# The order of a mixer's parts, and the beat of a scan behind weight splits

## The chip, the cores and the metric

The kernel runs on one core of a Trainium2 chip. The metric is the device time of one execution in microseconds (us). Three executions of the kernel before are compared; one further execution was profiled. TensorE (PE) does matrix products, VectorE (DVE) and ScalarE (ACT) elementwise work, GpSimd (POOL) some of it and the start of some transfers, SyncE (SP) the start of most others.

## What is computed

A network of two blocks on 256 tokens of width 1024. In the first block each of two layers has a feed-forward net, a mixer and another feed-forward net; the second block (attention, a dense net, eight experts) is not touched here. The mixer projects its input to many parts with one weight matrix, runs two branches and adds them through gates:

```python
def s5_branch(u, ...):                       # one of the two branches
    bu = einsum("blgc,gnc->blgn", ug, b_bar)             # complex input to 64 states
    _, states = associative_scan(combine, (a_elems, bu)) # s_t = lam_bar * s_(t-1) + bu_t
    y = real(einsum("blgn,gcn->blgc", states, c)) + d_skip * uf
    y = gelu(y)
    val, gate = split(y @ w_glu, 2)
    return val * sigmoid(gate)

def mixer(u, w_in, ...):
    proj = u @ w_in
    z, xbc, dt_raw, u5, g_a, g_b = split(proj, SPLITS)
    y_a = ssd_branch(z, xbc, dt_raw, ...) @ w_branch_a   # conv, silu, chunked scan, gate, norm
    y_b = s5_branch(u5, ...) @ w_branch_b
    merged = sigmoid(g_a) * y_a + sigmoid(g_b) * y_b
    return merged @ w_out
```

The SSD branch has four groups of heads. For each group a causal convolution and a silu give `xs`, a silu gives `zs`, a masked product over two chunks of 128 tokens gives `yT`, which is gated by `zs`, normed over the group's 512 columns and split for the product with `w_branch_a`.

## The kernel before

Matrix products run in fp32 with operands split in two: a weight tile `raw` of 128x1024 is loaded, ScalarE casts it to `hi` (line 1576) and VectorE makes `lo = raw - hi` (line 1577, `unit`). Three products (`hi*xh`, `lo*xh`, `hi*xl`, lines 1591 to 1593) stand for one. Such a tile with its two parts is called a unit here. Parts have a ring of buffers (`hi`/`lo` 0 to 2 and a pair called `part`), so ScalarE and VectorE can be at most four units ahead of TensorE in the stretch that matters here. A projection onto 512 columns (`stream_b`) is four units of 24 products, 96 in all, into four of five accumulators (`acc...`); the next projection needs them emptied, by ScalarE and VectorE.

The mixer's work is cut into parts, and `ORDER` says in which order they are written:

- `p0` to `p3`: the projections of SSD group 0 to 3 (`ssd_proj`), first 512 columns for `xs` (emptied by a ScalarE step at line 566, three convolution steps on VectorE at line 569, a silu), then 512 for `zs` (silu, line 642): eight units each. `accpa` is p0's accumulator, `accpb` p1's, `accpc` p2's, `accpd` p3's.
- `d`: the projection for dt, one small unit, and a chain of small VectorE steps on `cut` tiles.
- `g0` to `g3`: the projections of the gates, four units each (`accga` to `accgd`), with a tanh on ScalarE (line 753).
- `c0` to `c3`: the cores of SSD group 0 to 3 (`ssd_core`, `ssd_gate`; accumulators `trca` to `trcd`). A core transposes `xs`, builds for each of four head pairs a mask `M` (VectorE line 681, exp on ScalarE lines 688 and 689, VectorE line 690), multiplies it (lines 695, 696), then gates: `yT*zs` (VectorE 708), a square (ScalarE 710), two halving sums (GpSimd 713), a product with ones (TensorE 715), a power (GpSimd 720), a scaled identity `dg` (VectorE 724) and a product with it (TensorE 725). Each step needs the one before.
- `o0` to `o3`: S5's outputs for a quarter of its groups each: products into `zoa` to `zod` (lines 494 to 496, with coefficients `s5CF` loaded by GpSimd's queue), a gelu on ScalarE and VectorE, transposes (`troa` to `trod`, line 515), a split into `g`.

After `ORDER` follow the products with `w_glu` (`accgl`, which read the four `g`), `w_branch_b` (`accmb`), `w_branch_a` (`accma`). A scheduler then mixes the instructions: cores and outputs are put between the products of later projections, so that TensorE, which runs its queue in order, has other work while a core's chain runs on the other engines.

S5's recurrence (`s5_rec`) is 28 VectorE instructions on `S`, 14 for each half of the groups: six multiplications and additions of 128x1024 (line 545), two scans (line 549), six more. They are not written as one piece. `stream_b` calls `beside` after each unit, and `beside` puts one of them behind that unit's split:

```python
    def beside(self):
        with self.tc.issue_after(self.last_lo):
            next(self.side, None)
```

`o0` and `o1` need the first half, `o2` and `o3` the second. `MIXER` says which of the numbered buffers each kind of tile takes in turn; "X" serves the gates' tiles, S5's coefficients and its outputs, "W" (2 and 3) the recurrence's two temporaries `s5x`.

Of the kernel before, what the change touches and what calls it, by code (L numbers as in the profile page):

```python
# [27 lines left out]

ORDER = "p0 d p1 g0 g1 o0 o1 p2 c0 g2 c1 p3 o2 o3 g3 c2 c3".split()

MIXER = {
    "X": [2, 3, 0, 1], "U": [4, 5], "A": [12, 13, 6, 7, 8, 9, 10, 11, 12, 13, 6, 7, 8, 9, 6, 7], "M": [15, 16],
    "E": [10, 11, 14], "W": [2, 3],
    "bc": ["h0", "h1"], "T": ["h2", "h3"],
}
# [24 lines left out]
class Quads:  # L64


    def __init__(self, tiles):
        self.tiles = tiles
# [10 lines left out]
class Mixer:  # L79
# [471 lines left out]

    def beside(self):

        with self.tc.issue_after(self.last_lo):
            next(self.side, None)

# [231 lines left out]
    def mixer_body(self, I, l, xh, xl, hd):  # L788
        v = self.nc.vector
        W = I["w_in"][l]  # L790
        pr, ys = {}, []

        def proj(g):
            pr[g] = self.ssd_proj(W, l, g, xh, xl)

        def core(g):
            xs, zs = pr.pop(g)
            yT = self.ssd_core(l, g, xs, BC, acd, col)
            return self.ssd_gate(l, g, yT, zs)

        u = self.s5_in(W, xh, xl)
        self.ring_drop(("S", 0), ("S", 1), (6, 7))
        self.once = []
        St = self.qp.tile([P, 2, 32, 64], F32, tag="S", name=self.nm("S"), bufs=1)
        self.nc.gpsimd.memset(St[:, :, :, 0:1], 0.0)
        d = [self.s5_put(u[0])]
        BC = [self.ssd_bc(W, l, 0, xh, xl)]
        U = self.s5_get(d[0])
        d.append(self.s5_put(u[1]))
        E = self.s5_tables(l, 0, self.nc.sync)  # L810
        for q in range(2):
            self.s5_z(q, U[q], St)
        BC.append(self.ssd_bc(W, l, 1, xh, xl))
        U += self.s5_get(d[1])
        for q in range(2, 4):
            self.s5_z(q, U[q], St)
        self.side = itertools.chain(self.s5_rec(St, l, 0, E), self.s5_rec(St, l, 1))
        self.ring.append((12, 13))
        g5, ds, y23 = [], [], []
        for w in ORDER:  # L820
            k, i = w[0], int(w[1:] or 0)
            self.at = k + "abcd"[i]
            if k == "p":
                proj(i)
            elif k == "d":
                acd, col, cols = self.ssd_dt(W, l, xh, xl)
            elif k == "c":
                if i == 1:
                    self.ring_drop((12, 13))
                with self.tc.issue_after(self.last_mm):  # L830
                    if i == 0:
                        cols()
                    y = core(i)
                if i < 2:
                    ys.append(self.ssd_split(y))
                else:
                    y23.append(y)
            elif k == "g":
                ds.append(self.gate_out(W, i, xh, xl))
            elif k == "o":  # L840
                if i == 0:
                    self.ring_drop((8, 9))
                with self.tc.issue_after(self.last_mm):
                    self.s5_out(i, U[i], St, g5)
        self.at = "gl"
        bs = self.glu(I["s5_w_glu"][l], g5)
        self.at = "mb"
        ys += [self.ssd_split(y) for y in y23]
        yh, yl = Quads([y[0] for y in ys]), Quads([y[1] for y in ys])
        bh, bl = Quads([b[0] for b in bs]), Quads([b[1] for b in bs])  # L850
        mT = []
        for c in range(0, D, 256):
            if c % 512 == 0:
                mT.append(self.gate_back(ds[c // 512]))
            bb = self.stream_b(I["w_branch_b"][l][:, c : c + 256], bh, bl)
            for i in range(2):
                m = mT[-1][:, (c // P + i) % 4]
                v.scalar_tensor_tensor(m, m, 1.0, bb[i][:, :S], op0=ALU.add, op1=ALU.mult)
        self.ring = [0, 1, 2]
        self.ring_add([("S", 0), ("S", 1), (4, 5), (15, 16)])  # L860
        self.at = "ma"
        ms = []
        for c in range(0, D, 256):
            if c % 512 == 0:
                ms.append([self.slot4("X", "ms", F32R) for _ in range(2)])
                tg = self.gate_back(ds[2 + c // 512])
            ab = self.stream_b(I["w_branch_a"][l][:, c : c + 256], yh, yl, nk=16)
            for i in range(2):
                k = (c // P + i) % 4
                m, g = mT[c // 512][:, k], tg[:, k]  # L870
                v.scalar_tensor_tensor(g, g, 1.0, ab[i][:, :S], op0=ALU.add, op1=ALU.mult)
                v.tensor_tensor(m, m, g, op=ALU.add)
                self.split_half(ms[-1][0][:, k], ms[-1][1][:, k], m)
        h = [self.slot("B", "h") for _ in range(2)]
        for t in range(2):
            self.nc.sync.dma_start(h[t], hd[t * P : (t + 1) * P, :])
        return self.stream_k(I["w_out"][l], Quads([m[0] for m in ms]), Quads([m[1] for m in ms]), 8), h
# [545 lines left out]
class Net(Mixer, Second):  # L1423
    def __init__(self, ctx, tc):
        self.tc = tc
        nc = self.nc = tc.nc
        self.n = 0
        self.at = ""
        self.ring = [0, 1, 2]
        self.once = []  # L1430
        self.side = iter(())
        self.Ed = {}
        self.hold = []
        self.chain = [[], []]
        self.last_tr = None
        self.raws = itertools.repeat(None)

        def pool(name, bufs, **kw):
            return ctx.enter_context(tc.tile_pool(name=name, bufs=bufs, **kw))

        self.const = pool("const", 1)
        self.raw = pool("raw", 4)
        self.hi = pool("hi", 1)
        self.lo = pool("lo", 1)
        self.xp = pool("xp", 1)
        self.s4 = pool("s4", 5)
        self.qp = pool("numbered", 1)
        self.sm = pool("sm", 8)
        self.dram = pool("dram", 2, space=DRAM)
        self.acc = pool("acc", 5, space=PSUM)  # L1450
        self.trp = pool("trp", 2, space=PSUM)
        self.zp = pool("zp", 1, space=PSUM)

        self.ones = self.const.tile([P, P], F32, name="ones")
        nc.vector.memset(self.ones, 1.0)
        self.ident = self.const.tile([P, P], F32, name="ident")
        make_identity(nc, self.ident)
        self.mhalf = self.const.tile([P, 1], F32, name="mhalf")
        nc.vector.memset(self.mhalf, -0.5)
# [529 lines left out]
```

## Time and profile before

| | before |
|---|---|
| median of 3 runs | 2934.55 us (2931.49 to 2935.66) |
| profiled execution | 2936.55 us, span 2934.5 us |
| TensorE busy | 2814.3 us (96%), weight loads 2508.2 us (85%) |
| VectorE, ScalarE, GpSimd busy | 2181.6 us (74%), 1674.2 us (57%), 206.0 us (7%) |
| granted TensorE clock, mean | 0.981 of full speed |

TensorE is busy nearly all the time, so what can be won or lost is the idle time between its instructions, and stretches at the lower of its two clock levels. The mixer comes twice, once for each layer; the part around the change lies at 304 to 524 us and again at 1116 to 1337 us.

### The profile page before, as it was taken

Reading aid. Unit: us, or ns where it says so; the run is one execution under the profiler, and the core shown is the slowest. Engines: PE = TensorE matmul, PEld = TensorE weight load, DVE = VectorE, ACT = ScalarE, POOL = GpSimd, SP = SyncE. Lnnn points to the kernel's source line nnn. Section 1 sums busy time; section 2 is a strip of 40 time slices with the busy share of each in tenths; the row PEclk is TensorE's granted clock in tenths of the full one; section 3 lists DMA queues with packets and bytes.
Section 4 is the critical chain, followed back from the end, with each engine's and each line's share of the span. In section 5 each row is a group of like instructions: output and inputs, shape, how many; then the busy total and the mean of one; then the engine's idle time right before and its main releaser. Section 6 shows DMA issues by size and latency. Waiting matters only on the chain. (4 is left out here: it accounts for less than half of the span.)

```text
span 2934.5 us, 49144 instructions
## 1 busy us (share of the span) xinstructions
PE 2814.3 (96%) x19040; PEld 2508.2 (85%) x19040; DVE 2181.6 (74%) x3043; ACT 1674.2 (57%) x2389; POOL 206.0 (7%) x257
## 2 busy tenths in 40 slices
PE   8979999999999999999999999999999999999997
PEld 7968888999979888888999898987678888888886
DVE  5886877765667758777755566555589999999997
ACT  5434456545445444475554445445377777777776
POOL 2140001000004100010000000000000000000000
PEclk9999999999999999999999999999899999999998
DMA  7677565576567775656855646654589999999993
GB/s 238 199 250 242 160 204 164 197 227 188 184 223 249 241 221 174 194 155 196 264 171 180 215 154 192 186 192 132 184 279 356 343 361 361 343 359 356 354 344 145
DMA packets 350928, 687.88 MB, mean 234 GB/s; under 512 B 32672, under 2 KB 121952, under 8 KB 350688
## 3 DMA queue, kind: packets, MB, share of 16 engines
q1 hardware_dynamic: 336592, 637.42, 65.9%
q0 software_dynamic: 13952, 46.74, 4.8%
q8 instruction: 151, 2.47, 0.3%
q14 instruction: 89, 0.73, 0.1%
q10 hardware_dynamic: 144, 0.52, 0.0%
HBM read 658.05 MB, written 26.54 MB: 233 GB/s over the span
## 5 line engine op out<-in xcount | busy, mean ns | idle before, releaser
L1577 DVE TENSOR_TENSOR lo<-raw,hi 128x1024 fp32r<-128x1024 f32 x646 | 788.6, 1230 | 296.8 <-ACT hi L1576 285.1
L1576 ACT CAST hi<-raw 128x1024 fp32r<-128x1024 f32 x646 | 674.9, 1048 | 455.6 <-PE accmo L1587 84.6
L1586 PE MATMUL accmo<-lo,xg 128*128 128x512 f32 (+1 forms) x768 | 289.7, 378 | 2.3 <-DVE lo L1577 2.3
L1587 PE MATMUL accmo<-hi,xg 128*128 128x512 f32 (+1 forms) x768 | 285.2, 372 | 0.0
L1585 PE MATMUL accmo<-hi,xg 128*128 128x512 f32 (+1 forms) x768 | 274.0, 373 | 1.4 <-ACT hi L1576 1.4
L1577 DVE TENSOR_TENSOR big<-raw,big 128x1024 fp32r<-128x1024 f32 x147 | 184.9, 1259 | 110.2 <-ACT big L1576 109.3
L1576 ACT CAST big<-raw 128x1024 fp32r<-128x1024 f32 x147 | 153.7, 1049 | 168.0 <-issue 31.1
L1577 DVE TENSOR_TENSOR part<-raw,part 128x1024 fp32r<-128x1024 f32 x111 | 135.3, 1223 | 85.5 <-ACT part L1576 83.1
L1576 ACT CAST part<-raw 128x1024 fp32r<-128x1024 f32 x111 | 116.1, 1050 | 114.2 <-DMA raw<-in_ffn_w_gate_dram 17.4
L1586 PEld LDWEIGHTS accmo<-lo,xg 128*128 128x128 f32 x768 | 144.6, 188 | 32.3 <-DVE lo L1577 5.6
L1585 PEld LDWEIGHTS accmo<-hi,xg 128*128 128x128 f32 x768 | 144.6, 188 | 28.1 <-ACT hi L1576 2.6
L1587 PEld LDWEIGHTS accmo<-hi,xg 128*128 128x128 f32 x768 | 144.8, 189 | 22.5
L1586 PE MATMUL accmo<-lo,th 128*128 128x512 f32 x352 | 138.0, 392 | 0.0
L1587 PE MATMUL accmo<-hi,th 128*128 128x512 f32 x352 | 137.7, 391 | 0.0
L1577 DVE TENSOR_TENSOR lo<-big,hi 128x1024 fp32r<-128x1024 f32 x88 | 106.6, 1223 | 10.7 <-ACT hi L1576 7.6
L1585 PE MATMUL accmo<-hi,th 128*128 128x512 f32 x352 | 109.2, 391 | 0.0
L1576 ACT CAST hi<-big 128x1024 fp32r<-128x1024 f32 x88 | 92.7, 1054 | 27.0 <-PE accmo L1587 26.7
L1592 PE MATMUL accfa<-xh,lo 128*128 128x256 f32 x352 | 99.8, 284 | 0.0
L1591 PE MATMUL accfa<-xh,hi 128*128 128x256 f32 x352 | 99.7, 283 | 0.0
L1593 PE MATMUL accfa<-xl,hi 128*128 128x256 f32 x352 | 99.7, 284 | 0.0
L1577 DVE TENSOR_TENSOR lo<-more,hi 128x1024 fp32r<-128x1024 f32 x68 | 82.3, 1223 | 7.0 <-ACT hi L1576 5.0
L1576 ACT CAST hi<-more 128x1024 fp32r<-128x1024 f32 x68 | 71.4, 1053 | 19.3 <-PE accmo L1587 17.8
(993 smaller groups left out, 8603.3 us busy)
## 6 DMA issues: line engine op xcount, KB each, us to landing
raw<-in_w_gu_moe_dram SPq DMA_DIRECT2D x190, 512.0 KB, 5.3
raw<-in_w_in_dram SPq DMA_DIRECT2D x128, 512.0 KB, 4.4
raw<-in_w_down_moe_dram SPq DMA_DIRECT2D x94, 512.0 KB, 5.6
raw<-in_ffn_w_gate_dram SPq DMA_DIRECT2D x88, 512.0 KB, 4.1
raw<-in_ffn_w_up_dram SPq DMA_DIRECT2D x88, 512.0 KB, 4.3
raw<-in_ffn_w_down_dram SPq DMA_DIRECT2D x88, 512.0 KB, 4.2
big<-in_w_gu_moe_dram SPq DMA_DIRECT2D x60, 512.0 KB, 5.7
more<-in_w_gu_moe_dram SPq DMA_DIRECT2D x46, 512.0 KB, 5.7
```

Of the source, the lines that this page charges most:

```text
L1576: nc.scalar.copy(hi, raw)
L1577: self.last_lo = nc.vector.tensor_tensor(lo, raw, hi.bitcast(F32), op=ALU.subtract).ins
L1585: mm(ps, lh, rh, start=first, stop=False)
L1586: mm(ps, lh, rl, start=False, stop=False)
L1587: self.last_mm = mm(ps, ll, rh, start=False, stop=last).ins
L1591: mm(ps, lh, rh, start=first, stop=False)
L1592: mm(ps, ll, rh, start=False, stop=False)
L1593: self.last_mm = mm(ps, lh, rl, start=False, stop=last).ins
```

## The change

The order of the parts is another: `p2` and the third gate `g2` now come before S5's first outputs `o0 o1`, and the fourth gate `g3` comes between the cores `c0` and `c1`, no longer before `c2`. The recurrence has another beat: in the projections `p0`, `p1` (and `p3`) only each second unit takes an instruction of it along; `d`, the gates and `p2` still take one with each unit. The list of X buffers is reordered to suit.

```diff
-ORDER = "p0 d p1 g0 g1 o0 o1 p2 c0 g2 c1 p3 o2 o3 g3 c2 c3".split()
+ORDER = "p0 d p1 g0 g1 p2 g2 o0 o1 c0 g3 c1 p3 o2 o3 c2 c3".split()
...
-    "X": [2, 3, 0, 1], "U": [4, 5], "A": [12, 13, 6, 7, 8, 9, 10, 11, 12, 13, 6, 7, 8, 9, 6, 7], "M": [15, 16],
+    "X": [2, 3, 0, 1, 0] + [2, 3, 1, 0] * 5, "U": [4, 5], "A": [12, 13, 6, 7, 8, 9, 10, 11, 12, 13, 6, 7, 8, 9, 6, 7], "M": [15, 16],
...
     def beside(self):
 
+
+        self.beat += 1
+        if self.beat % self.pace:
+            return
         with self.tc.issue_after(self.last_lo):
             next(self.side, None)
...
         def proj(g):
+            self.pace = 1 if g == 2 else 2
             pr[g] = self.ssd_proj(W, l, g, xh, xl)
+            self.pace = 1
...
+        self.beat, self.pace = 0, 1
```

No instruction is added or taken away. By the written order, 25 of the 28 instructions of the recurrence stood behind the units of `p0 d p1 g0 g1` and the last 3 behind `p2`; now it is 17 (4, 1, 4, 4, 4), then 8 behind `p2` and 3 behind `g2`.

How the built program shows it, at three places, in the first layer. On VectorE, in the second half of p1 (`part_3834` and `lo_3865` before, `part_3819` and `lo_3850` now are its last two units; `cv` the convolution on p1's accumulators, `cut` the dt chain). Before:

```order
L1577 TENSOR_TENSOR part_3834<-raw_3832,part_3833 128x1024
L569 SCALAR_TENSOR_TENSOR cv_3734<-accpb_3606,cw,cv_3734 128x255
...
L545 TENSOR_TENSOR s5x_3805<-S_2763,s5E_3799 128x1024
L545 TENSOR_TENSOR s5x_3806<-S_2763,s5E_3800 128x1024
L103 TENSOR_SCALAR cut_3564<-cut_3564 32x256
L1577 TENSOR_TENSOR lo_3865<-raw_3863,hi_3864 128x1024
L569 SCALAR_TENSOR_TENSOR cv_3734<-accpb_3606,cw,cv_3734 128x254
...
L545 TENSOR_TENSOR S_2763<-S_2763,s5E_3799 128x1024
L104 TENSOR_SCALAR cut_3564<-cut_3564 32x256
L569 SCALAR_TENSOR_TENSOR cv_3734<-accpb_3606,cw,cv_3734 128x253
```

And now:

```order
L1584 TENSOR_TENSOR part_3819<-raw_3817,part_3818 128x1024
L545 TENSOR_TENSOR s5x_3285<-S_2763,s5E_2927 128x1024
L105 SCALAR_TENSOR_TENSOR cut_3560<-cut_3560 32x256
L573 SCALAR_TENSOR_TENSOR cv_3728<-accpb_3602,cw,cv_3728 128x255
...
L1584 TENSOR_TENSOR lo_3850<-raw_3848,hi_3849 128x1024
L106 SCALAR_TENSOR_TENSOR cut_3560<-cut_3560 32x256
L573 SCALAR_TENSOR_TENSOR cv_3728<-accpb_3602,cw,cv_3728 128x254
...
L107 TENSOR_SCALAR cut_3563<-cut_3560 32x256
L110 TENSOR_SCALAR cut_3560<-cut_3560 32x256
L573 SCALAR_TENSOR_TENSOR cv_3728<-accpb_3602,cw,cv_3728 128x253
```

Three multiplications of the recurrence stood between that unit and the end of the convolution; now it is one, with more steps of the dt chain.

On VectorE, in p2 (`lo_4261` is its fourth unit, `lo_4413` its eighth). Before, nothing of the recurrence stood behind p2's fourth unit; its last rows were these:

```order
L1577 TENSOR_TENSOR lo_4357<-raw_4355,hi_4356 128x1024
L545 TENSOR_TENSOR S_2763<-S_2763 128x1024
L1577 TENSOR_TENSOR part_4388<-raw_4386,part_4387 128x1024
L545 TENSOR_TENSOR S_2763<-s5x_3805,s5x_3806 128x1024
L1577 TENSOR_TENSOR lo_4419<-raw_4417,hi_4418 128x1024
L1577 TENSOR_TENSOR lo_4477<-raw_4475,hi_4476 128x1024
L1577 TENSOR_TENSOR lo_4507<-raw_4505,hi_4506 128x1024
```

And now:

```order
L1584 TENSOR_TENSOR lo_4261<-raw_4259,hi_4260 128x1024
L549 SCALAR_TENSOR_TENSOR S_2763<-s5E_4061,S_2763 128x1024
L1584 TENSOR_TENSOR lo_4320<-raw_4318,hi_4319 128x1024
L549 SCALAR_TENSOR_TENSOR S_2763<-s5E_4061,S_2763 128x1024
L1584 TENSOR_TENSOR lo_4351<-raw_4349,hi_4350 128x1024
L545 TENSOR_TENSOR s5x_4065<-S_2763,s5E_4059 128x1024
L1584 TENSOR_TENSOR part_4382<-raw_4380,part_4381 128x1024
L545 TENSOR_TENSOR s5x_4066<-S_2763,s5E_4060 128x1024
L573 SCALAR_TENSOR_TENSOR cv_4290<-accpc_4162,cw,cv_4290 128x255
...
L1584 TENSOR_TENSOR lo_4413<-raw_4411,hi_4412 128x1024
L545 TENSOR_TENSOR S_2763<-S_2763,s5E_4059 128x1024
```

The second half's two scans (they stand as rows of line 549) and its last turn have moved into p2.

On TensorE, from core 1's last mask product to S5's third transposes (`M_4945` and `M_5076` are the masks of its fourth head pair, `zs` its gate tile; `accgd` is the fourth gate, `accgl` the products with `w_glu`). Before:

```order
L696 MATMUL trcb_4955<-M_4945,xdt_4862 64x128
L1591 MATMUL accgd_5417<-xh_2478,hi_5450 128x256
...
L1593 MATMUL accgd_5418<-xl_2479,hi_5510 128x256
L1591 MATMUL accgl_5787<-g_575_4168,hi_5790 128x256
...
L715 MATMUL trcb_4963<-ones,zs_3605 128x1 x2
L1592 MATMUL accgl_5853<-g_575_4168,lo_5857 128x256
...
L725 MATMUL trcb_4971<-dg_4972,ones 128x128
L515 MATMUL troc_5326<-ident,y_747_5319 128x64 x4
L725 MATMUL trcb_4971<-dg_4975,ones 128x128
```

And now:

```order
L700 MATMUL trcb_5046<-M_5036,xdt_4993 64x128
L1598 MATMUL accgl_5787<-g_631_4580,hi_5790 128x256
...
L1600 MATMUL accgl_5854<-g_632_4581,hi_5856 128x256
L699 MATMUL trcb_5066<-M_5056,xdt_4993 64x256
...
L700 MATMUL trcb_5086<-M_5076,xdt_4993 64x128
L719 MATMUL trcb_5094<-ones,zs_3601 128x1 x2
L729 MATMUL trcb_5102<-dg_5103,ones 128x128
L515 MATMUL troc_5457<-ident,y_765_5450 128x64 x4
L729 MATMUL trcb_5102<-dg_5106,ones 128x128
```

Between core 1's last mask product and its product with ones stood 57 products of the fourth gate and 26 with `w_glu`, and 22 more before `dg`; now nothing stands there. The 48 products with `w_glu` that need only S5's first two outputs stand between the core's second and third head pair, and the fourth gate stands before the core begins. From about the first 80 products with `w_glu` on, TensorE's order is the same in both.

## Rows read from the trace of the kernel before

**Rows 1.** The page's first part: busy time, share of span, instructions.

```profile
PE 2814.3 (96%) x19040; PEld 2508.2 (85%) x19040; DVE 2181.6 (74%) x3043; ACT 1674.2 (57%) x2389; POOL 206.0 (7%) x257
```

**Rows 2.** Busy time by stretch: p1, g1, p2, steady products, core 1, a gap, layer 2's p1.

```profile
core 0: us, PE busy (x) PEld busy (x) DVE busy (x) ACT busy (x) POOL busy (x), PEclk, DMA share, GB/s
338.20:368.20 30.00, 25.86 (x194) 25.16 (x192) 29.69 (x46) 9.95 (x12) 1.06 (x2) 0.89 0.55 180
383.70:400.70 17.00, 13.79 (x98) 13.24 (x97) 16.49 (x14) 8.09 (x13) 0.75 (x2) 0.90 0.83 270
400.70:432.40 31.70, 31.22 (x401) 30.26 (x400) 19.60 (x31) 17.20 (x30) 2.67 (x5) 1.00 0.67 214
452.00:461.00 9.00, 9.00 (x77) 9.00 (x76) 6.51 (x9) 7.50 (x15) 2.98 (x2) 1.00 0.51 129
468.40:510.00 41.60, 38.59 (x449) 35.56 (x447) 29.84 (x50) 31.04 (x59) 6.02 (x7) 1.00 0.43 135
...
245.30:252.00 6.70, 6.09 (x18) 5.00 (x19) 6.57 (x11) 4.75 (x9) 0.55 (x1) 0.50 1.04 419
1150.00:1180.20 30.20, 25.81 (x193) 25.11 (x192) 29.89 (x46) 9.93 (x11) 1.07 (x2) 0.89 0.56 181
```

**Rows 3.** TensorE's waits, 304 to 524 us: total us, times, longest us.

```profile
PE accgb L1592 <- DVE lo L1577: 3.2, 2, 2.3
PE accpb L1592 <- DVE lo L1577: 2.6, 1, 2.6
PE accga L1591 <- ACT zs L642: 2.3, 1, 2.3
PE accpa L1592 <- DVE part L1577: 1.9, 1, 1.9
PE accpb L1591 <- DVE cv L569: 1.5, 1, 1.5
...
PE zoa L495 <- DMA s5CF<-Td: 0.5, 1, 0.5
```

**Rows 4.** VectorE in time in p0: start, duration, instruction, count.

```profile
322.25 2.29 DVE L549 TENSOR_TENSOR_SCAN S<-s5E,S 128x1024 f32<-128x1024 f32 x1
...
325.60 1.22 DVE L1577 TENSOR_TENSOR part<-raw,part 128x1024 fp32r<-128x1024 f32 x1
```

**Rows 5.** VectorE in time, second half of p1.

```profile
350.99 2.34 DVE L545 TENSOR_TENSOR s5x<-S,s5E 128x1024 f32<-128x1024 f32 x2
...
353.46 1.21 DVE L1577 TENSOR_TENSOR lo<-raw,hi 128x1024 fp32r<-128x1024 f32 x1
...
357.10 1.24 DVE L569 SCALAR_TENSOR_TENSOR cv<-accpb,cw,cv 128x253 f32<-128x253 f32 x3
```

**Rows 6.** VectorE in time, start of g1.

```profile
384.83 2.28 DVE L549 TENSOR_TENSOR_SCAN S<-s5E,S 128x1024 f32<-128x1024 f32 x1
387.04 1.20 DVE L1577 TENSOR_TENSOR lo<-raw,hi 128x1024 fp32r<-128x1024 f32 x1
```

**Rows 7.** Core 1 in time, from its second head pair to S5's third transposes.

```profile
481.77 0.42 PE L696 MATMUL trcb<-M,xdt 128*64 128x128 f32 x4
...
490.61 0.66 PE L695 MATMUL trcb<-M,xdt 128*64 128x256 f32 x4 [1.04 <-DVE M L690]
...
492.69 0.40 PE L696 MATMUL trcb<-M,xdt 128*64 128x128 f32 x4
...
503.20 2.18 POOL L713 TENSOR_TENSOR zs<-zs 128x512 f32<-128x512 f32 x2 [14.27 <-ACT zs L710]
505.51 0.53 PE L715 MATMUL trcb<-ones,zs 128*128 128x1 f32 x4
...
509.57 0.46 PE L515 MATMUL troc<-ident,y 64*128 64x64 f32 x4
```

**Rows 8.** Core 3 in time: last mask product, GpSimd's sums.

```profile
581.88 0.40 PE L696 MATMUL trcd<-M,xdt 128*64 128x128 f32 x4
...
586.98 2.72 POOL L713 TENSOR_TENSOR zs<-zs 128x512 f32<-128x512 f32 x2 [21.52 <-ACT zs L710]
```

## The prediction, made before the changed kernel ran

> **What bounds the kernel.** I read the page's busy shares first. TensorE is busy for 96% of the span [rows 1], so only two things can move the end: time in which TensorE stands idle, and time at the lower clock. Next I read the busy times by stretch [rows 2]. A steady stretch runs 77 products in 9.00 us, 0.12 us each, so p1's 192 products need 23.0 us and a gate's 96 need 11.5. p1's window has TensorE busy for 25.86 of 30.00 us: 4.1 us are idle and 2.8 of the busy time are lost to the clock, granted at 0.89 in the mean. g1's window has 3.2 idle and 2.3 lost, at 0.90. So where TensorE stumbles like this, each idle microsecond brings about 0.7 more through the clock (2.8/4.1 and 2.3/3.2). In both windows VectorE is the full engine: 29.69 of 30.00 and 16.49 of 17.00 us. In p2 it has room (19.60 of 31.70), and TensorE is idle there for only 0.5 us at full clock; core 1's window has 3.0 idle at full clock. Layer 2's p1 is like layer 1's (25.81 of 30.20, clock 0.89), so every sum below counts twice.
>
> The third view is TensorE's waits [rows 3]. The five longest groups make 11.5 us a layer and all lie in p0 to g1. Three are waits for VectorE's split (3.2, 2.6 and 1.9, together 7.7), one for a convolution that frees an accumulator (1.5), one for ScalarE's `zs` (2.3).
>
> **The change at the start (p0 to g2).** Eight instructions of the recurrence leave the stretch before p2. By number they are six of 1.2 us (the two multiplications of [rows 5] take 2.34) and two scans of 2.28 [rows 4, 6]: 11.8 us of VectorE. What this is worth I take wait by wait.
>
> - p0: before, a scan of 2.29 us ran shortly ahead of the split that TensorE then waited for [rows 4]. With half the beat it no longer stands there. I take the whole wait with its clock, 1.9 x 1.7 = -3.2 (bounds 0, if the raw weights' arrival sets the split, and -3.2).
> - p1: behind the unit concerned stood two multiplications, then a third, between the split and the convolution [rows 5]; the new order has one and more of dt's small steps. But scans come into p1's first half in place of multiplications, so VectorE reaches this place about as late as before. Half of the 2.6 us goes, -1.3 x 1.7 = -2.2; the 1.5 for the convolution stays (bounds 0 and 4.1 x 1.7 = -7.0).
> - g0: the wait is for ScalarE, whose order is the same. Nothing (bounds 0 and -2.3).
> - g1: a scan stands directly ahead of the split [rows 6], 2.28 against 1.2 for what takes its place, and one turn less is ahead of it. Of 3.2 us I leave 1.2: -2.0 x 1.7 = -3.4 (bounds 0 and -5.4).
>
> Sum -8.8. **p2 gets what left.** Before, p2 carried three instructions and ran between S5's outputs, whose products filled TensorE. Now it carries eight, two scans among them, has no outputs between its units, and looks as p1 looked before. I charge it a wait of 1.3 for its last split and 2.1 for the convolution to free a bank (VectorE must do its last three steps, 1.24 each [rows 5], behind the recurrence's), 3.4 x 1.7 = +5.8. Bounds: 0, as p2 is now, and p1's whole loss, 4.1 + 2.8 = +7.0. Of the queues, GpSimd's issues `s5CF`; the first load for `zoa` must follow the recurrence's last turn, which now stands behind g2's last unit, directly ahead of the outputs. Its wait of 0.5 [rows 3] I take at 1.1, +0.6 (bounds -0.5, and +1.8 with the longest wait of the list, 2.3). The start thus nets -8.8 + 5.8 + 0.6 = -2.4 a layer; with p1 unmoved and p2 at its bound about +1, with p2 clean -8.2.
>
> **The change at the end of core 1.** Before, core 1's chain ran under 57 products of the fourth gate and 48 with `w_glu`. Now the fourth gate is used up between S5's first outputs and core 0; between core 1's second and third head pair stand the 48 products (5.8 us), and behind its fourth pair nothing. TensorE's queue runs in order, so behind the waiting product with ones stand `dg`, S5's third transposes and everything with `w_glu` after them. Idle time by pieces:
>
> - Second to third head pair: before, 482.2 (the end of the four products begun at 481.77) to 490.61 is 8.4 us, and TensorE still waited 1.04 for VectorE's `M` at the end [rows 7]. So it was the chain's pace; with 5.8 covered, 2.6 are idle (bounds 1.0 and 2.6).
> - Last mask product to the end of GpSimd's sums: 493.09 to 505.4 in core 1 [rows 7], 12.4 us to the ones; in core 3, with less other work on VectorE and ScalarE, 582.28 to 589.70, 7.4 us [rows 8]. The 9.4 I take is nearer to core 3, since VectorE has no splits for a gate there any more (bounds 7.4 and 12.4).
> - Ones to S5's transposes: 4.06 us from start to start [rows 7], 2.6 of it 22 products with `w_glu`; the power on GpSimd and `dg` on VectorE must still run. Idle 2.5 (bounds 0.9, the 1.4 not covered by products less 0.5 of ones, and 3.5).
>
> That is 14.5 us; with the 2.0 of today's idle that is not the wait of 1.04, 16.5, less today's 3.0 and 0.5 of small work between, +13.0. After a hole of this size TensorE falls to the lower level: [rows 2] has 6.7 us at a granted 0.50, which is 1.2 GHz, behind an idle stretch. There that costs up to half, 3.4; I take 1.5 (bounds 0 and 3.4). The end of core 1 thus costs +14.5, between 1.0 + 7.4 + 0.9 - 3.0 = +6.3 and 2.6 + 12.4 + 3.5 + 2.0 - 3.0 + 3.4 = +20.9.
>
> The Trainium skill (TensorE: Matmul & The Clock Gate, section Why this matters for your kernels) asks that TensorE get no idle gaps between bursts of products, as it then falls to the lower level. That speaks against this change, and the granted 0.50 in [rows 2] agrees with it.
>
> **Sum.** -2.4 + 14.5 = +12.1 a layer, +24.2 in both. The profiled execution took 2936.55 us, 2.0 above the median of the runs shown; it would take 2960.8, and the median 2934.55 + 24.2, about 2959.
>
> **Rivals.**
> - The relief of VectorE counts in full, and core 1 goes at its lower bound: **faster**. For it speaks that VectorE is full in p1 and g1 and not in p2 [rows 2]. All waits for splits go, 7.7 x 1.7 = -13.1, p2 stays clean, +0.6 for `zoa`, +6.3 for core 1: -6.2 a layer, 2922 us. Against it: the instructions only move two projections on, and p1's chain of scans is in front of its units. It decides if core 1's hole is worth less than the start gives back: below about 8 us in all with p2 clean. Chance 0.12.
> - Both cancel: p2 clean (-8.2) and core 1 at +6.3 to +10, 2931 to 2938, about 2935. Chance 0.14, of which 0.08 within 0.2%.
> - Core 1 at its upper bound and the start at +1: VectorE and ScalarE are as busy with S5's outputs as today and the chain gets no faster: +21.9 a layer, 2978 us. Chance 0.12.
> - That the change doesn't do what it says holds in one place: with the split for g0 not what TensorE waits for, half the beat in p0 and p1 gives nothing there. This is in the sum.
>
> The Trainium skill (Perfetto Trace Analysis, section Identifying Performance Opportunities) says that improving means relieving the most contended engine. By that rule VectorE's 11.8 us would come back in full, twice, 2911 us; the first rival is this mechanism with its price from rows. TensorE's 96% [rows 1] speaks against the whole sum, as VectorE is the contended engine in some stretches alone.
>
> **How the numbers follow.** The forecast has 0.62; its own range is 2942 to 2972: start and core 1 together up to 8.5 us a layer less or 6.5 more than taken. Of the rivals, the first is faster by more than 0.2% (5.9 us, about what a measurement of this kernel can tell from no change), 0.12; the second gives 0.02 faster, 0.08 the same, 0.04 slower; the last is slower, 0.12. Faster 0.14, same 0.08, slower 0.78. The range leaves out the first rival and the outer half of the last: 2930 to 2976.
>
> **What the new profile would show.** The wait of `accpa` for `part` is gone; `accpb` keeps 2.5 to 4 us of waits, `accgb` about 1; `accpc` has new ones, some 3 us. In p2 VectorE is busy for over 90% and the granted clock is below 1. Core 1's product with ones has an idle stretch of 8 to 12 us ahead of it with GpSimd's sums as releaser, then a shorter one for `dg`, and a stretch at half clock follows. Wrong would be: no such idle stretch, so that some other work (the third outputs) filled it; or p2 without waits. If only the sizes differ, the hole ahead of the ones decides.

## The result, and the profile after

The changed kernel takes 2960.64 us (median; 2958.95 to 2965.21) against 2933.45 us for the kernel before in the same comparison: a ratio of 1.0097, 95% interval 1.0083 to 1.0111, about 28 us slower (the two medians differ by 27.2). The prediction said 2959, 24.2 us slower, range 2930 to 2976. The profiled execution takes 2961.25 us with a span of 2959.1, 24.6 above the span before.

The page's first part has 12 us more of TensorE's busy time than [rows 1], for the same 19040 products, so the clock has a share in the loss:

```profile
PE 2826.3 (96%) x19040; PEld 2518.4 (85%) x19040; DVE 2187.4 (74%) x3043; ACT 1676.8 (57%) x2389; POOL 204.0 (7%) x257
```

I cut each layer at the end of g1, since p0 to g1 hold the same TensorE work in both kernels, and follow it to the end of the products with `w_branch_b`. Busy times by stretch of the kernel before (layer 1 to g1, layer 1 from there, layer 2 likewise):

```profile
304.20:400.70 96.50, 84.36 (x700) 82.05 (x697) 89.15 (x122) 39.90 (x65) 3.25 (x6) 0.91 0.55 169
400.70:593.10 192.40, 184.73 (x1780) 173.74 (x1780) 139.02 (x238) 117.07 (x225) 24.55 (x32) 0.99 0.60 191
1116.00:1212.50 96.50, 84.08 (x698) 81.95 (x698) 89.17 (x122) 40.30 (x66) 3.26 (x6) 0.91 0.55 167
1212.50:1405.60 193.10, 184.68 (x1779) 173.68 (x1780) 140.73 (x240) 117.59 (x226) 25.95 (x33) 0.99 0.61 193
```

The same view of the changed kernel (columns as in [rows 2]), with p1 and p2 of layer 1, 17 us of p2 by themselves, four pieces around core 1, layer 2's p2, and then the four stretches:

```profile
330.90:360.10 29.20, 26.22 (x194) 25.52 (x192) 27.45 (x42) 9.94 (x12) 0.58 (x1) 0.88 0.54 168
...
390.30:418.40 28.10, 25.05 (x194) 24.64 (x194) 22.65 (x27) 12.93 (x20) 0.53 (x1) 0.94 0.54 159
...
391.70:408.70 17.00, 13.95 (x114) 13.54 (x113) 17.00 (x19) 6.41 (x10) 0.53 (x1) 0.99 0.77 241
...
493.80:504.00 10.20, 8.04 (x43) 7.28 (x40) 6.18 (x14) 9.07 (x23) 1.07 (x2) 0.50 0.09 28
504.00:510.80 6.80, 4.25 (x39) 3.70 (x38) 5.58 (x10) 6.14 (x11) 0.00 (x0) 1.00 0.43 116
510.80:527.70 16.90, 10.82 (x48) 9.36 (x49) 6.81 (x18) 6.18 (x16) 3.82 (x5) 0.50 0.20 62
527.70:538.40 10.70, 9.59 (x76) 8.69 (x74) 7.21 (x12) 4.21 (x7) 0.00 (x0) 0.99 0.19 53
...
1210.10:1238.10 28.00, 24.91 (x195) 24.50 (x194) 23.70 (x28) 13.02 (x20) 0.53 (x1) 0.94 0.59 178
300.40:390.30 89.90, 81.50 (x701) 79.42 (x699) 79.32 (x115) 39.91 (x65) 2.71 (x5) 0.94 0.58 177
390.30:602.60 212.30, 193.12 (x1779) 181.57 (x1779) 152.12 (x248) 118.90 (x226) 25.04 (x34) 0.93 0.55 176
1122.60:1210.10 87.50, 79.80 (x701) 77.84 (x699) 77.80 (x113) 40.01 (x65) 2.72 (x5) 0.96 0.59 177
1210.10:1428.20 218.10, 196.62 (x1780) 183.98 (x1779) 154.16 (x250) 119.12 (x226) 25.69 (x34) 0.91 0.55 174
```

The start wins 6.6 us in layer 1 (96.5 to 89.9) and 9.0 in layer 2, and VectorE has 10 to 11 us less to do there; in p1 it is busy for 27.45 of 29.20 us, no longer all the time. The rest of the layer loses 19.9 (192.4 to 212.3) and 25.0. That is 13.3 and 16.0 a layer, 29.3 in both; the profiled spans differ by 4.7 less, mostly because p0 already began 3.8 us earlier in this execution (300.4 against 304.2; in the twelve other profiles of this study it begins anywhere from 299.0 to 303.7).

TensorE's waits in layer 1 to 540 us (total, times, longest), which answer to [rows 3]:

```profile
PE trcb L719 <- POOL zs L717: 7.2, 1, 7.2
PE trcb L699 <- DVE M L694: 3.2, 1, 3.2
...
PE accgb L1599 <- DVE lo L1584: 2.2, 2, 1.3
PE accgl L1598 <- ACT zs L646: 2.2, 1, 2.2
PE accpb L1599 <- DVE lo L1584: 1.9, 1, 1.9
PE accpc L1598 <- DVE cv L573: 1.8, 1, 1.8
PE trcb L729 <- DVE dg L728: 1.5, 1, 1.5
PE accpc L1599 <- DVE lo L1584: 1.2, 1, 1.2
...
PE accpb L1598 <- DVE cv L573: 1.0, 1, 1.0
```

The wait of `accpa` for its part is gone, `accga` keeps its 2.3 for `zs`, and the others of the start are smaller; `accpc` has two new ones; and core 1 has four in a row. In layer 2 its largest are these:

```profile
PE trcb L719 <- POOL zs L717: 9.2, 1, 9.2
PE accgl L1598 <- ACT zs L646: 2.6, 1, 2.6
```

Core 1 in time in layer 1, the rows that answer to [rows 7]. The wait of 3.20 stands ahead of the first head pair, that of 2.16 (for an accumulator that ScalarE's `zs` still reads) between the second pair and the 48 products with `w_glu`; the third pair, at 506.68, waits for nothing. Then the chain can be followed from `yT*zs` through the square, the sums, the ones and `dg` to S5's third transposes. TensorE has nothing to do between them.

```profile
493.45 0.90 PE L699 MATMUL trcb<-M,xdt 128*64 128x256 f32 x4 [3.20 <-DVE M L694]
...
494.50 1.14 PE L699 MATMUL trcb<-M,xdt 128*64 128x256 f32 x4
...
498.22 0.58 PE L1598 MATMUL accgl<-g,hi 128*128 128x256 f32 x1 [2.16 <-ACT zs L646]
...
506.68 0.66 PE L699 MATMUL trcb<-M,xdt 128*64 128x256 f32 x4
...
510.91 1.22 DVE L712 TENSOR_TENSOR yT<-yT,zs 128x1024 f32<-128x1024 f32 x1
512.18 1.04 ACT L714 ACTIVATE zs<-yT 128x1024 f32<-128x1024 f32 x1
513.30 2.06 POOL L717 TENSOR_TENSOR zs<-zs 128x512 f32<-128x512 f32 x2 [9.33 <-ACT zs L714]
...
515.42 1.01 PE L719 MATMUL trcb<-ones,zs 128*128 128x1 f32 x4 [7.17 <-POOL zs L717]
...
517.89 0.77 PE L729 MATMUL trcb<-dg,ones 128*128 128x128 f32 x2 [1.46 <-DVE dg L728]
518.59 0.69 PE L515 MATMUL troc<-ident,y 64*128 64x64 f32 x4
```

### The profile page after: what moved, and what is told of

Same layout as the page of the kernel before. It is cut to its first block, busy times and chain, and to the rows that moved or that the text cites. A ratio compares the mean times of both kernels' runs of the same rounds, so it can differ in the third digit from the quotient of the medians.

```text
span 2959.1 us, 49159 instructions
## 1 busy us (share of the span) xinstructions
PE 2826.3 (96%) x19040; PEld 2518.4 (85%) x19040; DVE 2187.4 (74%) x3043; ACT 1676.8 (57%) x2389; POOL 204.0 (7%) x257
## 5 line engine op out<-in xcount | busy, mean ns | idle before, releaser
L1584 DVE TENSOR_TENSOR lo<-big,hi 128x1024 fp32r<-128x1024 f32 x88 | 106.5, 1222 | 10.8 <-ACT hi L1583 7.2
L1598 PE MATMUL accgl<-g,hi 128*128 128x256 f32 x256 | 78.3, 309 | 7.0 <-ACT zs L646 4.8
```

What stands on the lines that cost most here:

```text
L1584: self.last_lo = nc.vector.tensor_tensor(lo, raw, hi.bitcast(F32), op=ALU.subtract).ins
L1598: mm(ps, lh, rh, start=first, stop=False)
```

## The experiments

The first theory was the prediction's: the start wins about 9 us a layer, p2 pays 6 of it back, and core 1 costs about 15 since the fourth gate no longer lies under its chain. The rivals: S5's late outputs make the loss; the beat's scans make it; TensorE would have waited at the ones for something else anyway. Each kernel was compared with the kernel before in runs on the same chip (medians of before 2936.09, 2934.09 and 2935.48 us in the three groups).

| run | median us | ratio to before | 95% interval |
|---|---|---|---|
| the change | 2960.64 | 1.0097 | 1.0083 to 1.0111 |
| order alone | 2968.5 | 1.0113 | 1.0093 to 1.0134 |
| beat alone | 2946.4 | 1.0039 | 1.0026 to 1.0053 |
| outputs moved, new beat | 2939.9 | 1.0016 | 1.0005 to 1.0027 |
| outputs moved, old beat | 2944.68 | 1.0028 | 1.0015 to 1.0041 |
| change without core 1's sums | 2952.17 | 1.0050 | 1.0031 to 1.0070 |
| change, half beat in p2 too | 2957.66 | 1.0074 | 1.0061 to 1.0087 |
| change, gate behind core 1 | 2958.31 | 1.0076 | 1.0059 to 1.0093 |
| before, gate ahead of core 1 | 2946.57 | 1.0041 | 1.0026 to 1.0056 |
| before, half beat in p0 | 2935.04 | 1.0009 | 0.9997 to 1.0020 |
| the same, other buffers | 2935.69 | 0.9999 | 0.9989 to 1.0008 |
| before, half beat in p1, other buffers | 2938.39 | 1.0007 | 0.9998 to 1.0016 |
| before, two turns less in p0, other buffers | 2938.0 | 1.0005 | 0.9995 to 1.0015 |

The list of X buffers differs from that of the kernel before in every row but two ("gate ahead of core 1" and the first "half beat in p0"). The only pair that differs in the list alone, half beat in p0 with either list, shows no price for it (1.0009 and 0.9999, intervals overlapping); in the other orders the list was not tried by itself.

**Order alone.**

```diff
-            self.pace = 1 if g == 2 else 2
+            self.pace = 1
```

> The new order and the new list of buffers, with the old beat: one turn of the recurrence behind every unit. My theory: the start (p0 to g1) is as before the change again, so about 8 us a layer of relief are missing, p2 has three turns instead of eight and wins about 4 of its 5 us back, and core 1's idle stretches stay as in the changed kernel (14 us in its window). That is +3 to +5 a layer on the changed kernel: 2966 to 2972 us. The rival, that the beat costs time because two scans now stand in p2 and that this is the greater part of the loss, gives 2950 us or less.

Measured 1.0113, in the range of the theory. The waits of layer 1 show the start as it was before the change and core 1's hole in full:

```profile
PE trcb L719 <- POOL zs L717: 9.0, 1, 9.0
PE trcb L699 <- DVE M L694: 3.6, 2, 2.7
PE accgb L1599 <- DVE lo L1584: 3.2, 2, 2.3
```

The beat does not make the loss: the order, with its list of buffers, costs about as much as the whole change (the intervals overlap).

**Outputs moved, gates back.** The change with both gates where they stood before:

```diff
-ORDER = "p0 d p1 g0 g1 p2 g2 o0 o1 c0 g3 c1 p3 o2 o3 c2 c3".split()
+ORDER = "p0 d p1 g0 g1 p2 o0 o1 c0 g2 c1 p3 o2 o3 g3 c2 c3".split()
-    "X": [2, 3, 0, 1, 0] + [2, 3, 1, 0] * 5, ...
+    "X": [2, 3, 0, 1, 0, 0, 1, 1] + [2, 3, 0, 1] * 5, ...
```

> The new beat, and of the order only S5's first two outputs moved behind p2; the third and the fourth gate stand where they stood before the change. My theory: the loss hangs on the fourth gate's products no longer standing under core 1's chain, so here core 1 has no idle stretch above 2 us, the start has its relief, and p2 without outputs loses its 5 us as in the changed kernel: -2 to -4 a layer, 2925 to 2930 us. The rival, that the loss comes from S5's outputs being late (the products with w_glu wait for them), gives 2950 us or more, with waits of the products with w_glu for the parts of g.

Measured 1.0016 against the change's 1.0097: with the gates back (and the list of buffers that goes with them), some 24 of its 28 us are gone. Core 1's waits in layer 1:

```profile
PE trcb L699 <- DVE M L694: 2.6, 1, 2.6
PE accgd L1598 <- ACT zs L646: 2.6, 1, 2.6
...
PE trcb L719 <- POOL zs L717: 1.3, 1, 1.3
```

The wait at the ones is 1.3 in place of 7.2; the other two, 2.6 each, are more than the 2 us that the theory allowed core 1. And the time was expected at 2925 to 2930 and is 2940. The stretches of layer 1 to g1 and behind it say where that went:

```profile
300.50:389.80 89.30, 80.44 (x701) 78.46 (x698) 79.22 (x115) 39.98 (x66) 3.25 (x6) 0.96 0.59 180
389.80:594.40 204.60, 191.82 (x1780) 179.76 (x1779) 152.22 (x247) 118.16 (x225) 25.16 (x32) 0.96 0.57 181
```

The start is 7.2 us shorter than before, the rest 12.2 longer. So the start is shorter, and more than all of it is paid back behind g1.

**The same order with the old beat.** The pace is 1 everywhere, all else as in the run above.

> S5's first two outputs moved behind p2, with the old beat and the gates where they stood before the change: one move of the order alone. Theory A, that the beat only shifts VectorE's work and what the start wins p2 and p3 pay back: the start is as before (no relief), p2 with three turns waits under 1 us, so the time is within 4 us of the kernel with the same order and the new beat (2940): 2936 to 2944. Theory B, that the beat's relief is real and p2's loss comes from the missing outputs alone: p2 loses here too and the start wins nothing, +4 to +6 a layer on that kernel, 2948 us or more.

Measured 2944.68, just outside theory A's range and below theory B's; the intervals of the two beats overlap (1.0015 to 1.0041, 1.0005 to 1.0027). The two stretches:

```profile
299.30:394.40 95.10, 82.88 (x699) 80.60 (x699) 89.10 (x122) 39.90 (x65) 3.26 (x6) 0.93 0.55 170
394.40:594.40 200.00, 188.24 (x1780) 176.48 (x1778) 140.90 (x239) 117.54 (x225) 25.27 (x32) 0.97 0.58 185
```

The new beat takes 5.8 us from the start (95.1 to 89.3) and adds 4.6 behind g1 (200.0 to 204.6), with 9.9 us of VectorE's work moved and 11.3 added there. p2 without outputs but with three turns has one wait of 0.7, so theory B falls: p2's loss in the changed kernel is the recurrence's, not the missing outputs'. This run also prices the outputs' move, with the list of buffers that goes with it: 1.0028, about 8 us.

**Beat alone.** The order of before with the new beat; the list of buffers is that of the last two runs.

> The old order with the new beat (the buffers of S5's first two coefficient tiles and outputs are 0, 0, 1, 1, since the recurrence now runs on past them). My theory: core 1 has its cover again, no idle stretch ahead of its product with ones; the start keeps its relief of 7 to 9 us a layer; p2 has eight turns but also S5's products between its units, so it loses 1 to 3. Net -5 to -7 a layer: 2920 to 2925 us, faster than both kernels. The rival that p2 loses as much as in the changed kernel gives 2926 to 2930; the rival that the relief is only a shift of the waits gives 2933 or more.

Measured 1.0039, slower by 11 us: my theory fell here, the rival that the relief is a shift stands, and even that was too kind. The start wins nearly what was promised, 96.5 to 90.1 in layer 1, and the rest goes from 192.4 to 204.8:

```profile
301.10:391.20 90.10, 81.40 (x700) 79.20 (x698) 79.25 (x115) 39.78 (x65) 3.25 (x6) 0.94 0.59 179
...
391.20:596.00 204.80, 189.20 (x1780) 177.73 (x1780) 152.78 (x248) 117.20 (x225) 25.04 (x32) 0.97 0.58 182
```

Its largest new waits are spread over S5's outputs, p3 (3.0 for a split of `accpd`) and p2:

```profile
PE troc L515 <- DVE g L563: 3.1, 1, 3.1
...
PE accpc L1598 <- DVE cv L573: 2.5, 1, 2.5
```

S5's first outputs are among p2's units here, and p2 still waits 2.5 for the convolution. The buffers are a second edit in this run: the outputs no longer wait for the recurrence's last turn, come earlier among p2's units, and leave its last 77 products with none. How much of the 11 us is the beat's and how much the buffers' this run doesn't say.

**Gate ahead of core 1 in the kernel before.**

```diff
-ORDER = "p0 d p1 g0 g1 o0 o1 p2 c0 g2 c1 p3 o2 o3 g3 c2 c3".split()
+ORDER = "p0 d p1 g0 g1 o0 o1 p2 c0 g2 g3 c1 p3 o2 o3 c2 c3".split()
```

> The kernel before with one edit: the fourth gate from behind S5's last outputs to ahead of core 1, so core 1 runs under p3 and the outputs come with no gate. The beat and the place of the first outputs are as before the change. My theory: what counts is which work is left under the last chain ahead of the products with w_glu. Core 1 is done under p3, and the outputs' own chains (gelu, transposes, split) lie partly bare: 3 to 6 us a layer, 2940 to 2946 us, with waits at troc and trod and none above 2 us at the ones. The rival, that using up the fourth gate early costs the whole of the change's loss by itself, gives 2955 us or more.

Measured 1.0041, 12 us, at the theory's upper end (2946). Core 1's head pairs run under p3 here, its ones wait for nothing, and the loss is spread. But of the two waits that the theory named, `troc` has none and `trod` 0.9; the largest new ones are elsewhere:

```profile
PE trcb L699 <- DVE M L694: 3.0, 1, 3.0
PE accpd L1599 <- DVE lo L1584: 2.7, 1, 2.7
```

So using up the fourth gate early costs 12 us where core 1's head pairs still have p3's products. Where core 1 stands behind p3's end as well, the two kernels with the old beat differ by 25 (1.0028 to 1.0113), but there the third gate and the list of buffers moved too; no run moves the third gate alone.

**Gate behind core 1 in the changed kernel.**

```diff
-ORDER = "p0 d p1 g0 g1 p2 g2 o0 o1 c0 g3 c1 p3 o2 o3 c2 c3".split()
+ORDER = "p0 d p1 g0 g1 p2 g2 o0 o1 c0 p3 c1 g3 o2 o3 c2 c3".split()
```

> The changed kernel with the fourth gate moved from ahead of core 1 to behind it, and core 1 behind p3 (c0 p3 c1 g3). Then the fourth gate's products lie under core 1's first half, S5's last outputs and products with w_glu under its second. My theory: the idle stretch ahead of the ones shrinks from 7.2 to 0 to 3 us, the rest is as in the changed kernel: -8 to -12 a layer, 2937 to 2945 us. The rival, that TensorE then runs out of work for S5's last outputs or that core 0 lies bare under p3, gives 2950 or more with idle stretches of over 5 us at troc or trca.

Measured 1.0076, 2958 us: the theory (2937 to 2945) fell, and the time is the rival's (2950 or more), though core 0's wait is 4.1 where the rival had over 5. The hole is as long as in the changed kernel:

```profile
PE trcb L719 <- POOL zs L717: 7.2, 1, 7.2
```

The scheduler put the gate's products under core 0's last steps and ahead of core 1's masks, and the `w_glu` products that are ready between core 1's head pairs; behind its last mask product one product was left. What covers a chain is the work that TensorE's order has at that point, and the written order of the parts doesn't say it.

**Without core 1's sums.** Group 1's norm sums over a quarter of its columns.

```diff
-        for n in (512, 256):
+        for n in (512, 256) if g != 1 else ():
```

> The changed kernel with core 1's two halving sums on GpSimd left out (so the norm of group 1 sums over a quarter of its columns). My theory: the idle stretch ahead of core 1's product with ones is the length of the chain square, sums, ones, so it gets shorter by the sums' 2.2 us: 7.2 to about 5.0, and the kernel by 2 to 3 us a layer with the clock: 2955 to 2957 us. The rival, that TensorE would have had to wait there anyway for something else (the splits or the gelu of S5's last outputs), leaves the time at 2959 to 2962 and puts the wait on another tile.

The wait at the ones becomes 5.2 with the square as its releaser, as the theory had it:

```profile
PE trcb L719 <- ACT zs L714: 5.2, 1, 5.2
```

So the chain's length is what TensorE waits for, and in layer 1 no other wait takes its place. The time is 2952.17, 8 us less than the change (14 by the ratios, whose intervals don't meet), more than the expected 4 to 6. That the clock gave the rest was not separated.

**Half the beat in p2 as well.** The third projection takes every second turn too; the list of buffers is adapted.

> The changed kernel with half the beat in p2 as well, so that four turns stand behind p2's units, four behind the third gate's and three behind the fourth's (the buffers of S5's first outputs are 1, 1, 0, 0). My theory: p2's waits (1.8 for the convolution, 1.2 for a split) fall to under 1.5 together, the third gate takes one or two in their place, and the rest is as in the changed kernel: -1 to -4 a layer, 2953 to 2959 us. The rival, that p2's waits come from the missing outputs between its units and not from the recurrence, leaves them and the time as they are: 2959 to 2962.

Measured 1.0074, the median 3 us under the change's, in the expected range. p2's wait for the convolution falls from 1.8 to 0.7 and that for the split rises from 1.2 to 1.7, 2.4 together where under 1.5 was expected; the wait at the ones is 8.6 in place of 7.2. The intervals of the two just overlap, so this is weak support that the turns make p2's waits.

**Smaller reliefs in the order of before.** Half the beat in p0 alone:

> The kernel before with half the beat in p0 alone; the order, the buffers and every other beat are its own, so four turns move from p0 to p2. My theory: the wait of accpa for its part (1.9 us) goes, those of p1 and g1 shift by up to 1 us, p2 stays under 1 us of waits because S5's products stand between its units: -2 to -5 a layer, 2924 to 2930 us. The rival, that the waits move on into p1 and p2, gives 2931 to 2936.

With the buffers 0, 0, 1, 1 for S5's first coefficients and outputs:

> The old order with half the beat in p0 alone, as in the run before, but with the buffers 0, 0, 1, 1 for S5's first coefficient tiles and outputs, so that the coefficients no longer wait for the recurrence's last turn. In the run before, the first outputs waited 2.4 us for them. Theory: that wait goes, the rest stays: -2 to -3 a layer on that run, 2928 to 2932 us, and faster than the kernel before by 2 to 6. The rival, that the coefficients' wait only covered another (p2's units or the second tile's load, which now has one buffer less), leaves 2933 to 2937.

Half the beat in p1 alone, the same buffers:

> The old order, half the beat in p1 alone, the same buffers 0, 0, 1, 1. p1 is the stretch in which VectorE was fullest, so if its relief counts there, p1's waits (2.6 for a split, 1.5 for the convolution) shrink by 2 us or more, while p0 keeps its 1.9; four turns move to p2. If what is taken from the start is paid back one for one, the time is 2933 to 2938 us; if the relief is kept because p2 has room for seven turns, 2926 to 2930.

p0's last two units without a turn, the same buffers:

> The old order and beat, but p0's last two units take no turn along, so the first two scans stand behind dt's unit and p1's first, and all that follows is two turns later; the same buffers 0, 0, 1, 1. Theory: p0's wait of 1.9 with its clock goes, g1 has the second half's two scans behind its second and third unit (wait as before, 2 to 4 us), p2 with five turns stays under 1 us of waits: -1 to -3 a layer, 2928 to 2932 us. The rival, that the work only shifts and shows again in p1 or g1, gives 2933 to 2937.

None of the four can be told from the kernel before (0.9999 to 1.0009, all intervals hold 1). Each time the waits moved on. Half the beat in p0 took away `accpa`'s wait, left `accpb` with 2.7 and made S5's coefficients late:

```profile
PE zoa L495 <- DMA s5CF<-Td: 2.4, 1, 2.4
```

With the other buffers that wait went to the second set of coefficients (3.2 at `zob`), as the rival had it. With half the beat in p1, `accpb`'s wait for the split fell to 1.0, and 3.3 stood at `zob`. With two turns less in p0, `accpa`'s wait went, `accpb` kept 2.7, and 3.2 stood at core 1's `dg`. No version of the study beats the kernel before.

## Why the prediction held

- **p0, p1, g0, g1: -8.8 a layer; measured -6.6 and -9.0.** `accpa`'s 1.9 is gone, as said. The waits of `accpb` are 2.9 in layer 1, within the 2.5 to 4 expected; `accga` keeps its 2.3, as said; `accgb` keeps 2.2 where I left 1.2. p0 to g1 have 0.94 and 0.96 of the clock in place of 0.91, and their TensorE busy time falls by 2.9 and 4.3 us while idle time falls by 3.7 and 4.7: 0.8 to 0.9 of clock for each idle microsecond, where I had 0.7.
- **p2: +5.8; measured +5.1 and +5.0** (28.1 and 28.0 us against 23.0). The two waits named came at 1.2 and 1.8 for 1.3 and 2.1. That VectorE would be busy for over 90% there was wrong over p2 as a whole: it is 81% (22.65 of 28.10 us). But in the 17 us from 391.7 to 408.7, in which both waits lie, it is busy for 17.00 us; the idle time comes after them.
- **S5's coefficients: +0.6; measured 0.** `zoa` waits for nothing: the recurrence's last turn ends at 422.8, GpSimd's queue issues the load at 423.1, it lands within 4.8 us, and TensorE is busy with g2 until 429.9.
- **Core 1: +14.5; measured 14.8 in layer 1 and 20.0 in layer 2** (the loss behind g1 less p2's). In layer 1 it lies there: the granted clock is 1.00 from 418.4 to 488.0 and from 538.4 to 602.6, with 1.0 us of idle time in both together. By pieces: between the second and third head pair 2.6 was expected, and 2.2 and 2.6 came, but not by the mechanism. It was to be the chain's pace, a wait for the third pair's `M`; TensorE waited for an accumulator, ahead of the `w_glu` products, and the third pair then waited for nothing. In layer 1 another 3.2, for `M`, stands ahead of the first pair, where the prediction had none. At the ones 9.4, measured 7.2 and 9.2; for `dg` 2.5, measured 1.5 twice. The forecast pieces thus came to 10.8 and 13.3 against 14.5, and with the 3.2 layer 1 has 14.0.
- **The term that was mis-sized is the clock behind core 1, with the idle time it stood beside.** I had +13.0 of idle time and +1.5 of clock. Behind g1, TensorE's idle time grows from 7.7 to 19.2 us, its busy time from 184.7 to 193.1; without p2's 3.0 and 2.0, core 1 is +8.5 idle and +6.4 clock in layer 1, and +10.0 and +10.0 in layer 2. The clock falls at the first of the four waits, not after the last, and it falls twice. Four mask products take 0.90 us right behind the wait of 3.20, against 0.66 in [rows 7]; the granted clock is 0.50 from 493.8 to 504.0, so the 48 products with `w_glu` that were to cover 5.8 us took 8.5. It is 1.00 again from 504.0, falls within the wait ahead of the ones and is 0.50 from 510.8 to 527.7. TensorE is busy for 18.9 us of these two stretches (8.04 and 10.82), where the prediction had one of at most 6.7. The idle time is smaller partly since the small waits that stood behind core 1 before are gone from the list: after a hole the products with `w_glu` find their splits done. Those of before, in its list of waits:

```profile
PE accgl L1592 <- DVE lo L1577: 1.3, 2, 0.9
...
PE trod L515 <- DVE g L559: 1.2, 1, 1.2
```

The two errors nearly cancel in layer 1, which is luck; layer 2 is 5 us worse than layer 1, partly by waits of p3 and core 0 of 0.4 to 1.2 us that layer 1 has less of. Why it has them stays open. That the median came out within 2 us of 2959 is luck as well: by the stretches the two layers lose 29.3 where the sum had 24.2.

Of the rivals, the first (relief counts in full) fell on the price of core 1, and the runs with the gates back show that it would have fallen without it: the relief is paid back behind g1. The second (both cancel) had p2 clean and core 1 at 10 at most, and neither came. The last had core 1 at +20.9, which layer 2 nearly reached (20.0). That the relief of VectorE should be kept by a stretch with room (19.60 of 31.70 us in p2, [rows 2]) was not what these runs showed. The rule of the most contended engine (Trainium skill, Perfetto Trace Analysis, section Identifying Performance Opportunities), which the prediction read so that VectorE's 11.8 us count in full, is not borne out in this reading for work that is only moved. The rule against idle gaps between bursts (Trainium skill, TensorE: Matmul & The Clock Gate, section Why this matters for your kernels) is borne out: 0.50 granted behind the wait of 3.2 and from within that of 7.2 on, and 6 to 10 us a layer of busy time.

In sum, from kernels that differ by one step each (the first two bring their lists of buffers along): S5's outputs behind p2 about +8 us (1.0028), the two gates' new places about +25 (to 1.0113), the new beat about -5 (to 1.0097, intervals overlapping). The stretch behind g1 in layer 1 tells the same in its order: +7.6 us, +16.6 (209.0 against 192.4), and +19.9 with the new beat, which takes 5.3 from the start (95.2 to 89.9). The prediction had no term for the outputs' move apart from p2's and that of S5's coefficients; with the old beat, where p2 waits for only 0.7, it costs those 7.6.

## What to carry to other kernels

When parts are reordered, look for the longest chain of dependent small steps and ask, in the built order of the engine that executes in order, which products stand between its first and its last step; a part that covers it cannot be spent elsewhere, and where it is written in the source doesn't tell. Price each hole with the clock of what runs behind it, the short ones ahead of the long one too, and take off the small waits behind it that it swallows. Work moved off a full engine to a later stretch is relief only if that engine isn't full where the moved work lands; its busy share over the whole stretch doesn't tell.

## What the runs showed of the hardware

The clock's share was larger than I had thought, and it came in two pieces. In layer 1 of the changed kernel TensorE's clock fell to its lower level (0.50 granted, 1.2 GHz) right behind the wait of 3.2 us, at 493.8, and 48 products of 128x256 took 8.5 us in place of 5.8. It was at full level again at 504.0, behind products that ran without a wait from 498.2 on. It fell a second time at 510.8, within the wait of 7.2 us, and was back at 527.7, behind products that ran without a wait from 517.9 on. A mean hides this: over the 34.8 us from 498.2 to 533.0 the granted clock is about two thirds, and TensorE is busy for 73% of them. Where VectorE was relieved the clock rose as well, from 0.91 to 0.94 and 0.96 over 90 us.
